# Scratch and queue places for the sums of the normed x in a decoder trunk on one core

## The chip, the cores and the metric

The kernel runs on one core of one Trainium2 chip. The metric is the device time of one execution in microseconds. Before the change it is 1301.23 us, the median of 3 runs (1300.35 to 1301.33). The engines are named as the profile names them: PE (TensorE, with PEld for its weight loads), DVE (VectorE), ACT (ScalarE), POOL (GpSimd) and SP (SyncE, whose queue issues the loads).

## The reference

Four sub-layers follow each other on a residual stream of 512 tokens and 1024 channels, all in float32: a gated MLP with position mixing, a squared-ReLU MLP, forgetting attention, and a second squared-ReLU MLP. The change touches the two squared-ReLU MLPs:

```python
h = rms_norm(x, mlp_norm_g[i])                      # x * rsqrt(mean(x*x)) * gain
x = x + jnp.square(jax.nn.relu(h @ w1)) @ w2         # w1: 1024 x 4096, w2: 4096 x 1024
```

## The kernel before

The stream is kept transposed: x is 8 tiles of 128 channels by 512 tokens. A float32 product is made of three matmuls of a reduced format: each operand is split into a high part (a copy that rounds, on ACT) and a low part (the remainder, on DVE), and high x high, high x low and low x high are added. Names that end in h and l are such parts: xh and xl of the normed x (without its scale per token), wh and wl of a chunk of weights, zh and zl of the MLP's inner activations.

**The norm.** Class Norm makes xh and xl of a block of x with its gain, squares the block on ACT (sq) and adds the squares up on POOL (sqs, line 283). When all 8 blocks are there, finish multiplies the sum by ones on PE (nps), and makes rstd on POOL (line 295); spread broadcasts rstd over the partitions with 4 matmuls (npb), copied by ACT to rbc. rbc is what the inner activations are scaled with.

**The MLP.** mlp handles w1 in pairs of chunks of 128 columns. The pairs 0 and 1 are made plainly (ph_0 to ph_3: 24 matmuls 512 wide for each chunk). nps stands after ph_1 and npb after ph_2 on PE. All later pairs are made by a scheme of 7 half-sized products instead of 8 (up_pair, PSUM tiles da and bc), in which two operands are needed as sums and differences:

- of the normed x: token_sums(k) for k = 0 to 3 takes the blocks k and k + 4 of x with gain (two copies on ACT, tx, line 466), makes four sums of 128 x 256 on POOL (ts, lines 470 to 473), and splits them (th on ACT, line 474; tl on DVE, line 475). They are made once for an MLP and serve all its pairs. Line 471 adds to the result of line 470, and line 473 to that of line 471.
- of the weights: Stream._sums makes four sums of 128 x 512 for each pair on POOL (ssum, lines 110 to 113) and splits them (sh, sl).

Both kinds of sums take their scratch from one tag, ssum, with two buffers: token_sums(k) takes both, one for tx and one for ts, and the sums of one pair of weights take both. The inner activations zh and zl have tags of their own with five buffers each.

Weights come through three raw buffers of 512 KB, loaded by SP in the order of use. A raw buffer is free for the next load when its split and its sums are made.

**What sets the order.** The kernel is written as a dataflow; a scheduler with a timeline of its own puts each engine's instructions in an order at build time, and every engine then works its own list in that order. Calls on keep_in_program_order pin a few matmuls (the first of ph_2 and of ph_3, and some in up_pair). In the program's text, token_sums stands after the plain pairs; the sums of weights of pair 2 come as soon as its chunks are asked for ahead of use.

## Time and profile before

| | |
|---|---|
| median of the runs | 1301.23 us |
| profiled execution, its own time | 1301.62 us |
| its span, first to last instruction | 1299.7 us |
| PE busy | 1273.0 us, 98% of the span |
| DVE, ACT, POOL busy | 867.9, 631.4, 511.3 us |
| PE's share of the chain that ended last | 85% |
| start of the first MLP in the span | about 289 us |
| start of the second MLP | about 941 us |

PE's busy time is modelled from pipelined matmuls and is no measure of its peak; the pace from one matmul's start to the next one's is. A row of the waits has the waiting engine and line, what it waited for, the sum in us, how many times, and the longest. A row of the chain has its start, its length and the engine, tile and line. A row of the timeline has start, duration, engine, line, operation, and in brackets the idle time before it with what ended it. The names there lack their numbers.

### The profile page before, as it was taken

Reading aid. Unit: us, or ns where it says so; the run is one execution under the profiler, and the core shown is the slowest. Engines: PE = TensorE matmul, PEld = TensorE weight load, DVE = VectorE, ACT = ScalarE, POOL = GpSimd, SP = SyncE. Lnnn points to the kernel's source line nnn. Section 1 sums busy time; section 2 is a strip of 40 time slices with the busy share of each in tenths; the row PEclk is TensorE's granted clock in tenths of the full one; section 3 lists DMA queues with packets and bytes.
Section 4 is the critical chain, followed back from the end, with each engine's and each line's share of the span. In section 5 each row is a group of like instructions: output and inputs, shape, how many; then the busy total and the mean of one; then the engine's idle time right before and its main releaser. Section 6 shows DMA issues by size and latency. Waiting matters only on the chain.

```text
span 1299.7 us, 18573 instructions
## 1 busy us (share of the span) xinstructions
PE 1273.0 (98%) x7204; PEld 1124.9 (87%) x7204; DVE 867.9 (67%) x1196; ACT 631.4 (49%) x992; POOL 511.3 (39%) x440
## 2 busy tenths in 40 slices
PE   9999999998999999999999999999988999999998
PEld 8888888887899999998899899998867999999987
DVE  7347767685676676766637777777875867676763
ACT  6234323255544343433467687787454534344430
POOL 4118533026433232310657567675285323222200
PEclk9999999999999999999999999999998999999999
DMA  6233232321332423233223222323212333332321
GB/s 240 88 111 98 82 94 85 97 83 49 115 114 80 130 79 117 90 106 94 75 83 102 81 82 79 93 68 112 81 49 84 113 112 96 100 111 85 114 82 65
DMA packets 39495, 124.01 MB, mean 95 GB/s; under 512 B 4688, under 2 KB 5728, under 8 KB 39408
## 3 DMA queue, kind: packets, MB, share of 16 engines
q1 hardware_dynamic: 39232, 122.82, 29.8%
q8 instruction: 56, 0.92, 0.3%
q14 instruction: 31, 0.25, 0.1%
q0 software_dynamic: 32, 0.02, 0.0%
q10 hardware_dynamic: 144, 0.00, 0.0%
HBM read 120.69 MB, written 2.13 MB: 95 GB/s over the span
## 4 chain that ended last, share of the span: by engine, by line
PE 85%; DVE 7%; POOL 3%; ACT 3%; issue 2%; DMA 0%; SPq 0%; POOLq 0%; DVEq 0%; ACTq 0%
PE po L241 34%; PE da L241 12%; PE bc L241 9%; PE pq L241 8%; PE pu L241 7%; PE pv L241 7%; PE pg L241 2%; DVE xl L269 2%; PE ot L241 2%; PE lg L241 1%; PE tp L246 1%; DVE wl L86 1%; PE sp L421 1%; DVE tl L475 1%; ACT wh L85 1%
## 5 line engine op out<-in xcount | busy, mean ns | idle before, releaser
L85 ACT ACTIVATE wh<-raw 128x1024 fp32r<-128x1024 f32 (+3 forms) x230 | 219.0, 953 | 284.2 <-PE po L241 80.8
L86 DVE TENSOR_TENSOR wl<-raw,wh 128x1024 fp32r<-128x1024 f32 (+1 forms) x178 | 250.5, 1419 | 75.2 <-ACT wh L85 73.4
L241 PE MATMUL po<-zl,wh 128*128 128x512 f32 x512 | 200.5, 392 | 0.0
L241 PE MATMUL po<-zh,wh 128*128 128x512 f32 x512 | 200.2, 391 | 0.0
L241 PE MATMUL po<-zh,wl 128*128 128x512 f32 x512 | 199.5, 390 | 0.0
L552 DVE TENSOR_TENSOR x<-x,po 128x512 f32<-128x512 f32 x128 | 87.3, 683 | 106.8 <-PE po L241 106.7
L86 POOL TENSOR_TENSOR wl<-raw,wh 128x768 fp32r<-128x768 f32 (+3 forms) x52 | 102.4, 1970 | 125.6 <-ACT wh L85 123.0
L110 POOL TENSOR_TENSOR ssum<-raw 128x512 f32<-128x512 f32 x28 | 38.1, 1359 | 246.2 <-DMA raw<-in_m_dram 216.7
L85 ACT ACTIVATE sh<-ssum 128x1024 fp32r<-128x1024 f32 x56 | 59.4, 1060 | 152.8 <-POOL ssum L111 112.1
L241 PEld LDWEIGHTS po<-zh,wl 128*128 128x128 f32 x512 | 96.3, 188 | 19.6
L241 PEld LDWEIGHTS po<-zh,wh 128*128 128x128 f32 x512 | 96.4, 188 | 18.0
L241 PEld LDWEIGHTS po<-zl,wh 128*128 128x128 f32 x512 | 96.5, 189 | 16.3
L241 PE MATMUL pq<-wh,xh 128*128 128x384 f32 (+2 forms) x256 | 88.4, 345 | 0.0
L405 POOL TENSOR_SCALAR vn<-v,mv,lnr 128x128 f32<-128x128 f32 x64 | 63.3, 1002 | 59.4 <-DVE vl L409 59.3
L241 PE MATMUL pq<-wh,xl 128*128 128x384 f32 (+2 forms) x256 | 83.1, 325 | 0.0
L241 PE MATMUL pq<-wl,xh 128*128 128x384 f32 (+2 forms) x256 | 82.7, 323 | 0.0
L86 DVE TENSOR_TENSOR sl<-ssum,sh 128x1024 fp32r<-128x1024 f32 x56 | 71.1, 1271 | 14.6 <-ACT sh L85 14.6
L112 POOL TENSOR_TENSOR ssum<-raw,ssum 128x512 f32<-128x512 f32 x28 | 42.2, 1507 | 78.4 <-DVE sl L86 78.2
L241 PE MATMUL da<-th,sl 128*128 128x256 f32 x224 | 63.4, 283 | 0.0
L241 PE MATMUL da<-tl,sh 128*128 128x256 f32 x224 | 63.4, 283 | 0.0
L241 PE MATMUL da<-th,sh 128*128 128x256 f32 x224 | 63.1, 282 | 0.0
L241 PE MATMUL pv<-wh,xl 128*128 128x512 f32 (+1 forms) x160 | 58.6, 372 | 0.5 <-DVE xl L269 0.5
(212 smaller groups left out, 3534.2 us busy)
## 6 DMA issues: line engine op xcount, KB each, us to landing
raw<-in_m_dram SPq DMA_DIRECT2D x128, 512.0 KB, 3.6
raw<-in_gw_u_dram SPq DMA_DIRECT2D x16, 512.0 KB, 3.5
raw<-in_gw_o_dram SPq DMA_DIRECT2D x16, 512.0 KB, 3.5
raw<-in_fw_qkv_dram SPq DMA_DIRECT2D x20, 384.0 KB, 3.0
raw<-in_gw_v_dram SPq DMA_DIRECT2D x14, 512.0 KB, 3.6
raw<-in_fw_g_dram SPq DMA_DIRECT2D x8, 512.0 KB, 3.4
cb<-cd SPq DMA_DIRECT2D x16, 256.0 KB, 3.3
raw<-in_fw_o_dram SPq DMA_DIRECT2D x8, 512.0 KB, 3.5
```

Source lines behind the costliest of these rows:

```text
L85: self.nc.scalar.activation(hi, t, AF.Copy)
L86: eng.tensor_tensor(lo, t, hi.bitcast(F32), op=ALU.subtract)
L110: tt(s12[:, 0], a21, a22, op=ALU.add)
L112: tt(s43[:, 0], a12, s12[:, 1], op=ALU.subtract)
L241: ins = pe.matmul(dst, a, b, start=start, stop=stop, skip_group_check=more)
L246: placed(pe.transpose(dst, src, ident[: src.shape[0], : src.shape[0]]), 256)
L269: dve.scalar_tensor_tensor(l, x[b], gcol, h.bitcast(F32), op0=ALU.mult, op1=ALU.subtract)
L405: pool.tensor_scalar(vn[:, i], v[i][:, cb * P : (cb + 1) * P], mv[:, i, 0:1], lnr[:, i : i + 1], op0=ALU.subtract, op1=ALU.mult)
L421: pe.matmul(dst, vh[:, 2 * c + i], wide, start=True, stop=False)
L475: dve.tensor_tensor(tl[k], t, th[k].bitcast(F32), op=ALU.subtract)
L552: dve.tensor_tensor(x[b], x[b], pt, op=ALU.add)
```

## The change

token_sums takes its two scratch tiles from the tags zh and zl (five buffers each) and no longer from ssum, so that the four rounds have eight tiles of their own. Its four rounds are moved in the text ahead of the plain pairs, and are queued behind the norm's last square on ACT and its last sum on POOL: issue_after(i) adds an edge of order, with no wait, from i to each instruction of the block that runs on i's engine. The first sums of weights after them are queued behind the last token sum on POOL in the same way.

```diff
-        self.sums_pool = None
+        self.sums_pool = self.sums_behind = None
...
         if kind == "second":
-            self._sums(i, self.raw.pop(i - 1)[0], t)
+            with self.sums_behind or nullcontext():
+                self._sums(i, self.raw.pop(i - 1)[0], t)
+            self.sums_behind = None
...
-            act.activation(sq, x[b], AF.Square)
+            self.squared = [act.activation(sq, x[b], AF.Square)]
...
-                pool.tensor_tensor(s, self.sum, sq, op=ALU.add)
+                self.squared.append(pool.tensor_tensor(s, self.sum, sq, op=ALU.add))
...
             def token_sums(k):
-                xg, t = (mp.tile([P, 2, S], F32, tag="ssum", name=f"t{w}{nm.n}_{k}", bufs=2) for w in "xs")
+                xg, t = (mp.tile([P, 2, S], F32, tag=f"z{w}", name=f"t{w}{nm.n}_{k}", bufs=5) for w in "hl")
...
-                tt(t[:, 3], b21, t[:, 1], op=ALU.subtract)
+                last = tt(t[:, 3], b21, t[:, 1], op=ALU.subtract)
                 act.activation(th[k], t, AF.Copy)
                 dve.tensor_tensor(tl[k], t, th[k].bitcast(F32), op=ALU.subtract)
+                return last
...
             zs = {}
+            with ExitStack() as behind:
+                for ins in nm.squared:
+                    behind.enter_context(tc.issue_after(ins.ins))
+                for k in range(4):
+                    last = token_sums(k)
+            ws.sums_behind = tc.issue_after(last.ins)
             phs = [up(0), up(1)]
             nm.finish()
...
             zs[1] = squares(1, more)
-            for k in range(4):
-                token_sums(k)
```

The change moves instructions on all engines at the start of each MLP; from the fourth pair on the lists are the same again. Three places matter here, all at the start of the first MLP.

POOL before, from the norm's last sum (sqs_7) into the second round of token sums. ssum are sums of weights, tx the x with gain, ts the sums:

```order
L283 TENSOR_TENSOR sqs_7_2452<-sqs_6_2430,sq_7_2450 128x512
L111 TENSOR_TENSOR ssum_0_2546<-ssum_0_2546,raw_2354 128x512
L112 TENSOR_TENSOR ssum_1_2547<-raw_2354,ssum_0_2546 128x512
L470 TENSOR_TENSOR ts_0_2639<-tx_0_2638 128x256
L472 TENSOR_TENSOR ts_0_2639<-tx_0_2638 128x256
L471 TENSOR_TENSOR ts_0_2639<-tx_0_2638,ts_0_2639 128x256
L295 TENSOR_TENSOR rstd_2537<-ms_2535,mhalf 128x4
L473 TENSOR_TENSOR ts_0_2639<-tx_0_2638,ts_0_2639 128x256
L470 TENSOR_TENSOR ts_1_2649<-tx_1_2648 128x256
```

And after the change, the end of the token sums (the scratch is now named th and tl as the split parts are, and is told from them by its 256 columns; lines from the second on are moved by 2):

```order
L475 TENSOR_TENSOR tl_0_2469<-th_0_2468,tl_0_2469 128x256
L472 TENSOR_TENSOR tl_3_2499<-th_3_2498 128x256
L474 TENSOR_TENSOR tl_3_2499<-th_3_2498 128x256
L473 TENSOR_TENSOR tl_2_2489<-th_2_2488,tl_2_2489 128x256
L475 TENSOR_TENSOR tl_1_2479<-th_1_2478,tl_1_2479 128x256
L473 TENSOR_TENSOR tl_3_2499<-th_3_2498,tl_3_2499 128x256
L475 TENSOR_TENSOR tl_2_2489<-th_2_2488,tl_2_2489 128x256
L297 TENSOR_TENSOR rstd_2577<-ms_2575,mhalf 128x4
L475 TENSOR_TENSOR tl_3_2499<-th_3_2498,tl_3_2499 128x256
L112 TENSOR_TENSOR ssum_0_2586<-raw_2404 128x512
```

sqs_7 now stands 8 token sums ahead of the first of these rows, with no sum of weights around it. The rounds are interleaved; the last sum of round 0 is the ninth of 16. rstd stands behind 15 token sums, where it stood behind three, and the sums of weights of pair 2 behind all 16. In the second MLP rstd stands behind 13, where it stood behind four.

ACT after the change, from the norm's last square (sq_7) to the copy of the broadcast rstd (rbc):

```order
L280 ACTIVATE sq_7_2450<-x_104 128x512
...
L468 ACTIVATE th_3_2498<-x_104,gains 128x512
L85 ACTIVATE wh_2542<-raw_2354 128x1024
L476 ACTIVATE th_0_2460<-tl_0_2469 128x1024
L85 ACTIVATE wh_2582<-raw_2404 128x512
L476 ACTIVATE th_1_2461<-tl_1_2479 128x1024
L476 ACTIVATE th_2_2462<-tl_2_2489 128x1024
L476 ACTIVATE th_3_2463<-tl_3_2499 128x1024
L85 ACTIVATE wh_2634<-raw_2509 128x1024
L306 ACTIVATE rbc_2629<-npb_2624 128x512
L85 ACTIVATE sh_0_2592<-ssum_0_2586 128x1024
```

The eight copies with gain follow sq_7 (seven of the eight are left out); before, sh_0 and sh_1 and a split of weights (wh) followed it, and the copies came two by two between the splits th. The splits of the sums of weights come after rbc now.

PE after the change, from the last matmul of ph_3 on:

```order
L243 MATMUL ph_3_2631<-xh_7_2446,wl_2512 128x512
L243 MATMUL da_2_2704<-th_0_2460,wh_2582 128x256
L243 MATMUL da_2_2704<-tl_0_2464,wh_2582 128x256
L243 MATMUL da_2_2704<-th_0_2460,wl_2583 128x256
L243 MATMUL da_2_2704<-th_1_2461,wh_2582 128x256
L243 MATMUL da_2_2704<-tl_1_2465,wh_2582 128x256
L243 MATMUL da_2_2704<-th_1_2461,wl_2583 128x256
L243 MATMUL da_2_2704<-th_2_2462,wh_2582 128x256
```

Pair 2's first product now runs through all four rounds; before, matmuls of bc_2 on xh and xl, and from there on of pair 3, stood between th_0 and th_1, and between th_1 and th_2.

## The prediction

> **What bounds the kernel now.** The page first: TensorE (PE) is busy nearly all of the span and holds most of the chain that ended last, so only a stretch in which PE stands still can give time back.

> ```profile
> span 1299.7 us, 18573 instructions
> PE 1273.0 (98%) x7204; PEld 1124.9 (87%) x7204; DVE 867.9 (67%) x1196; ACT 631.4 (49%) x992; POOL 511.3 (39%) x440
> ```

> Then the waits from 300 to 330 us, the start of the first MLP, and from the chain one round of what it names there:

> ```profile
> ACT th L474 <- POOL ts L473: 10.6, 4, 3.9
> POOL ts L470 <- DVE tl L475: 7.5, 3, 2.5
> PE da L241 <- ACT th L474: 5.2, 3, 4.0
> ...
> 309.77 0.74 POOL ts L470
> 310.52 0.70 POOL ts L472
> 311.21 1.70 POOL ts L471
> 312.97 0.75 POOL ts L473
> 313.74 1.07 ACT th L474
> 314.83 1.24 DVE tl L475
> ...
> 316.20 0.74 POOL ts L470
> ```

> PE waits for the split of the normed sums (th), that for POOL's sums (ts), and POOL for DVE's remainder (tl) of the last round: the scratch has two buffers and each round takes both, so the four rounds run one after another, 6.4 us each (309.77 to 316.20). What PE loses comes from the windows of PE alone (length, busy and count, clock, DMA), for both MLP starts, with its pace from the chain (12 narrow matmuls in 1.43 us, 17 wide ones in 3.89):

> ```profile
> 313.10:329.20 16.10, 9.95 (x55) 0.79 0.00 1
> 317.50:321.60 4.10, 0.07 (x1) 0.76 0.00 0
> 321.60:326.30 4.70, 4.69 (x22) 0.50 0.00 0
> 970.20:989.50 19.30, 13.47 (x86) 0.82 0.11 30
> 982.30:988.50 6.20, 5.86 (x25) 0.50 0.23 67
> ...
> 337.58 3.89 PE po L241 x17
> 341.70 1.43 PE da L241 x12
> ```

> All matmuls in the two long windows are narrow, 0.12 us each. First: 16.10 - 55 x 0.12 = 9.5 us lost. Second: 19.30 - 86 x 0.12 = 9.0. Part of it is no wait: after standing for 4 us PE ran at a granted clock of 0.50 for 4.70 us, where 22 matmuls should take 2.6 (2.1 lost).

> **The change, removed.** With a scratch tile for each round no round waits for the last one's tl, and all 16 sums follow each other. The ceiling is 9.5 + 9.0 = 18.5 us. The first real zh and zl take the fifth slots; the second pair takes slots free since tl_0, long before: nothing.

> **Moved on ACT.** Eight copies now stand right behind the last square. A pair took 1.32 us with its end, so eight take about 5. They fall into a hole, ACT's wait for the first sum of weights:

> ```profile
> 291.95 0.62 ACT L278 ACTIVATE sq<-x 128x512 f32<-128x512 f32 x1
> 298.33 1.06 ACT L85 ACTIVATE sh<-ssum 128x1024 fp32r<-128x1024 f32 x1 [5.76 <-POOL ssum L111]
> 301.61 1.32 ACT L466 ACTIVATE tx<-x,gains 128x512 f32<-128x512 f32 x2
> ```

> They end at 292.5 + 5 = 297.5, and the split of weights behind them, which before stood behind this sh and a second one, comes earlier. Without the hole it would be 5 us later. Cost: nothing.

> **Moved on POOL: the price.** The order shows that rstd, which PE needs for the broadcast npb, now stands behind 15 of the 16 sums in the first MLP and 13 in the second; before, behind 3 and 4. How long 15 sums take depends on DVE:

> ```profile
> 310.47 0.74 POOL L472 TENSOR_TENSOR ts<-tx 128x256 f32<-128x256 f32 x1
> 310.58 1.71 DVE L86 TENSOR_TENSOR wl<-raw,wh 128x1024 fp32r<-128x1024 f32 x1 [0.95 <-ACT wh L85]
> 311.17 1.73 POOL L471 TENSOR_TENSOR ts<-tx,ts 128x256 f32<-128x256 f32 x1
> 295.77 1.28 POOL L283 TENSOR_TENSOR sqs<-sqs,sq 128x512 f32<-128x512 f32 x1
> 305.56 1.02 POOL L295 TENSOR_TENSOR rstd<-ms,mhalf 128x4 f32<-128x4 f32 x1
> 306.64 0.60 PE L241 MATMUL npb<-ident,rstd 128*128 128x128 f32 x3 [0.32 <-POOL rstd L295]
> 291.41 1.54 DVE L86 TENSOR_TENSOR wl<-raw,wh 128x1024 fp32r<-128x1024 f32 x1
> ```

> A sum alone takes 0.70; DVE's wl began beside one, ended 1.1 after it, and the next sum ended 0.6 after that: the two engines take turns. So I walk the first start by turns. Last square done 292.6, wl done 292.95, sqs_7 (1.25) 294.2, xl_7 (0.6) 294.8, six sums 299.0, wl of the next chunk (1.1) 300.1, three sums 302.2: now round 0 is whole; th_0 (1.07) 303.3, meanwhile two sums 303.6, tl_0 (1.15) 304.75, one sum, half a wl (0.6), three sums 308.15. There tl_1 waits too. If rstd goes first it ends at 309.2, else at 310.3. PE reaches npb at 306.3, so it waits 2.9 to 4.0 and npb comes 2.6 to 3.7 later than at 306.64; I take 3.2.

> The second start has a cover for this:

> ```profile
> 944.94 1.85 DVE L269 SCALAR_TENSOR_TENSOR xl<-x,gains,xh 128x512 fp32r<-128x512 f32 x1
> 951.82 3.95 POOL L283 TENSOR_TENSOR sqs<-sqs,sq 128x512 f32<-128x512 f32 x2
> 955.82 1.05 PE L241 MATMUL nps<-ones,sqs 128*128 128x2 f32 x8 [1.47 <-POOL sqs L283]
> 963.91 0.83 PE L241 MATMUL npb<-ident,rstd 128*128 128x128 f32 x6
> ...
> PE ph L241 <- DVE xl L269: 1.6, 2, 0.9
> ```

> There the four sums of weights stood between the norm's squares and held sqs_7 to 955.8. With them behind, xl_5 (0.6 from 944.94) frees DVE and POOL at 945.6, and sqs_5, a wl, sqs_6, xl_6 and sqs_7 follow by turns (1.2 + 1.15 + 1.2 + 0.6 + 1.2) to 950.9. Then xl_7 (0.6), 13 sums (9.1), one and a half wl (1.75), perhaps tl_0 (1.15), and rstd (1.02), which ends at 963.4 or 964.5: npb stays within 0.6 of 963.91. PE, which waits less for xl and not for sqs_7, starts nps at about 953.2, and these (0.9) and 24 wide matmuls (5.5) bring it to npb at 959.6. It waits 3.9 to 4.9 there: the 4.3 us won ahead of npb are all given back. I take 0.

> **The clock after such a wait.** PE stood 2.0 us ahead of 975.30 and kept its clock, 3.5 ahead of 982.30 and 4.0 ahead of 321.6 and lost it:

> ```profile
> 975.30 0.39 PE L241 MATMUL da<-th,wh 128*128 128x256 f32 x1 [2.00 <-ACT th L474]
> 982.30 0.58 PE L241 MATMUL da<-th,wh 128*128 128x256 f32 x1 [3.50 <-ACT th L474]
> ```

> The new wait of the second start is over that bound: ph_3's wide matmuls at half clock for some 4.7 us lose about 2.2. That of the first lies astride it: I take half, 1.1. [...]

> **Sums of weights and loads, later.** The first sums of pair 2 stood here:

> ```profile
> 291.82 2.28 POOL L110 TENSOR_TENSOR ssum<-raw 128x512 f32<-128x512 f32 x1
> ```

> The four now start at about 310 and take some 7 us; their splits follow on ACT and DVE by 320.4. PE comes for them 36 narrow matmuls (4.3 us) after ph_3, at 319 or later. SP's loads of the next two chunks wait for them as well, where before one waited for a wl; they land 3.6 us after:

> ```profile
> raw<-in_m_dram SPq DMA_DIRECT2D x128, 512.0 KB, 3.6
> ```

> One place runs short: ACT's copy of an early product stands behind a split that waits for such a load, 0.6 us in each start by my walk. Without the cover of those 36 matmuls it would be 4.3 more.

> **Sum.** First 9.5 - 3.2 - 1.1 - 0.6 = 4.6. Second 9.0 - 0 - 2.2 - 0.6 = 6.2. Together 10.8 us off the profiled execution's 1301.62 (span 1299.7 and 1.9 around it), 1290.8; the median shown is 0.4 lower, so **1290.5**.

> **Rivals.** *rstd in time:* it goes ahead of tl_1 and the clock holds in both. First 9.5 - 2.6 - 0.6 = 6.3, second 9.0 + 0.5 - 0.6 = 8.9: 1286. For it: the short wait of the first start; against: 3.9 us in the second. With no turns taken at all (0.70 a sum) rstd ends at 305.7 and 961.0, the gains are 8.9 and 11.2, and the time is 1281, the lower bound.

> *Slower, POOL's queue ahead of npb:* with a mean of m us a sum, the first start gains 18.2 - 15m and the second 18.2 - 13m, half clock in both. At m = 1.73, the slowest row above, that is -7.8 and -4.3: 1313. It decides from m = 1.30. Against it, the 16 sums of each start as they ran:

> ```profile
> 302.30:326.80 24.50, 15.67 (x16) 0.86 0.14 43
> 956.90:981.20 24.30, 15.85 (x16) 0.93 0.14 44
> ```

> 0.98 and 0.99 each, which would give 9.0 and 1292. They had gaps in which DVE could work; now they have none.

> *The stall only changes its name:* m near 1.3, or PE runs dry at the sums of weights, 5 us in each start: about 1301. For it: POOL's work is the same. Against: POOL stood idle for 7.5 us between the rounds, and that goes.

> **How the numbers follow.** Forecast 0.66 (alone 1287 to 1294), rstd in time 0.20, name only 0.08, slower 0.06. The range reaches from near the bound without turns to just short of no change: 1283 to 1297. A measurement of this kernel can tell about 0.2%, 2.6 us: faster 0.86, same 0.08, slower 0.06.

> **What would show it.** Right: no wait of POOL for tl; both long windows full; PE waiting at npb for rstd, 3 to 4 us and 4 to 5 us, with a clock near 0.5 after the second. Wrong in the price: npb within 1 us of when ph_2 ends. Wrong altogether: waits of da or bc for sh or sl of 4 us and more in pairs 2 and 3, or rstd later than 312.

## The result and the profile after

The changed kernel takes 1291.23 us (median of 4 runs, 1290.36 to 1292.59) against 1300.79 us before (4 runs). The ratio is 0.9928, with a 95% interval of 0.9915 to 0.9940. The prediction was 1290.5 us, within 1283 to 1297.

From the page of the changed kernel, its span:

```profile
span 1290.8 us, 18568 instructions
```

The busy shares of the engines tell nothing of the change: PE has 98% as before. The waits of PE do, from 284 to 345 us, and behind the line of dots from 935 to 1000 us. (Lines of the code are two higher than before; tl on POOL's lines 472 to 475 is the scratch of the token sums, and th on ACT's line 468 is their x with gain.)

```profile
PE npb L243 <- POOL rstd L297: 3.1, 1, 3.1
PE po L243 <- ACT wh L85: 1.2, 1, 1.2
PE bc L243 <- ACT sl L526: 1.1, 1, 1.1
PE da L243 <- DVE zc L508: 0.4, 1, 0.4
...
PE npb L243 <- POOL rstd L297: 4.0, 1, 4.0
PE po L243 <- ACT wh L85: 0.7, 1, 0.7
```

PE's waits for th and tl are gone (for th 5.2 us in the part of the first start that was shown). In their place stands one wait for rstd in each start, 3.1 and 4.0 us, and in the first start three late ones, 2.7 us together.

The windows of PE alone show what these waits did to the clock: the wait and what stands behind it to the end of ph_3 in the first start, then the same in the second, with the part at half clock by itself (length, busy and count, clock, DMA).

```profile
305.96:309.04 3.08, 0.00 (x0) 1.00 0.00 0
309.04:315.51 6.47, 6.47 (x32) 1.00 0.15 36
956.29:960.30 4.01, 0.00 (x1) 0.89 0.00 0
960.30:966.01 5.71, 5.71 (x17) 0.50 0.00 0
960.30:969.58 9.28, 9.28 (x33) 0.68 0.17 49
```

Behind the wait of 3.08 us the clock stayed at 1.00. Behind that of 4.01 it was 0.50 for 5.71 us, and npb to the end of ph_3 took 9.28 us where it took 6.37 before (963.91 to 970.28).

Where the time came from is read by anchors on PE that both kernels have: the first ph of each MLP, and between them the first pq of the attention. The rows are PE's timeline, of before and then of the change:

```profile
288.88 0.39 PE L241 MATMUL ph<-xh,wh 128*128 128x512 f32 x1
644.88 0.35 PE L241 MATMUL pq<-wh,xh 128*128 128x400 f32 x1
941.12 0.39 PE L241 MATMUL ph<-xh,wh 128*128 128x512 f32 x1
```

```profile
288.52 0.39 PE L243 MATMUL ph<-xh,wh 128*128 128x512 f32 x1
641.05 0.34 PE L243 MATMUL pq<-wh,xh 128*128 128x400 f32 x1
937.73 0.39 PE L243 MATMUL ph<-xh,wh 128*128 128x512 f32 x1
```

| stretch | before | change | gain |
|---|---|---|---|
| ahead of the first MLP | 288.88 | 288.52 | 0.36 |
| first MLP | 356.00 | 352.53 | 3.47 |
| attention | 296.24 | 296.68 | -0.44 |
| second MLP to the end | 358.58 | 353.07 | 5.51 |
| span | 1299.7 | 1290.8 | 8.9 |

The new bound of the start is in the chain of waits of the change, from the norm's last sum to the third of the sums of weights of pair 2 (start, length, what):

```profile
292.37 1.37 POOL sqs L285
293.73 1.15 POOL tl L472
...
307.01 1.98 POOL rstd L297
...
313.45 2.25 POOL ssum L113
```

From 292.37 to 315.70 it is POOL, piece on piece with no gap. All engines in that stretch, of before and of the change (length; then busy and count of PE, PEld, DVE, ACT and POOL; clock, DMA):

```profile
293.70:326.00 32.30, 27.20 (x136) 23.09 (x135) 16.65 (x17) 17.51 (x22) 21.78 (x22) 0.90 0.16 49
```

```profile
293.70:326.00 32.30, 27.64 (x158) 23.74 (x157) 20.28 (x18) 16.69 (x23) 30.65 (x26) 1.00 0.16 50
```

POOL's busy time, its waits inside an instruction among it, went from 21.78 to 30.65 of 32.30 us. The engine that stood idle between the rounds has become the full one.

### The profile page after: what moved, and what is told of

Read it like the earlier page. It is cut to its first block, busy times and chain, and to the rows that moved or that the text cites. A ratio compares the mean times of both kernels' runs of the same rounds, so it can differ in the third digit from the quotient of the medians.

```text
span 1290.8 us, 18568 instructions
## 1 busy us (share of the span) xinstructions
PE 1269.8 (98%) x7204; PEld 1123.9 (87%) x7204; DVE 878.7 (68%) x1196; ACT 630.0 (49%) x992; POOL 515.1 (40%) x440
## 4 chain that ended last, share of the span: by engine, by line
PE 86%; DVE 5%; POOL 4%; ACT 3%; issue 1%; DMA 0%; POOLq 0%; ACTq 0%; DVEq 0%
PE po L243 34%; PE da L243 12%; PE bc L243 9%; PE pq L243 8%; PE pv L243 7%; PE pu L243 7%; PE pg L243 2%; DVE xl L271 2%; PE ot L243 2%; PE tp L248 1%; PE lg L243 1%; PE sp L423 1%; DVE ee L809 1%; ACT wh L85 1%; POOL tl L473 1%
## 5 line engine op out<-in xcount | busy, mean ns | idle before, releaser
L85 ACT ACTIVATE wh<-raw 128x1024 fp32r<-128x1024 f32 (+3 forms) x230 | 219.1, 953 | 282.1 <-PE po L243 85.3
L86 DVE TENSOR_TENSOR wl<-raw,wh 128x1024 fp32r<-128x1024 f32 (+1 forms) x178 | 256.4, 1453 | 59.9 <-ACT wh L85 59.4
L86 POOL TENSOR_TENSOR wl<-raw,wh 128x768 fp32r<-128x768 f32 (+3 forms) x52 | 102.4, 1969 | 126.4 <-ACT wh L85 123.8
L85 ACT ACTIVATE sh<-ssum 128x1024 fp32r<-128x1024 f32 x56 | 59.4, 1060 | 161.7 <-POOL ssum L113 116.8
L86 DVE TENSOR_TENSOR sl<-ssum,sh 128x1024 fp32r<-128x1024 f32 x56 | 72.6, 1296 | 9.9 <-ACT sh L85 9.8
L114 POOL TENSOR_TENSOR ssum<-raw,ssum 128x512 f32<-128x512 f32 x28 | 39.5, 1409 | 76.7 <-DVE sl L86 76.5
L115 POOL TENSOR_TENSOR ssum<-raw,raw 128x512 f32<-128x512 f32 x28 | 63.0, 2252 | 0.0
## 6 DMA issues: line engine op xcount, KB each, us to landing
raw<-in_m_dram SPq DMA_DIRECT2D x128, 512.0 KB, 3.6
raw<-in_gw_u_dram SPq DMA_DIRECT2D x16, 512.0 KB, 3.6
raw<-in_gw_o_dram SPq DMA_DIRECT2D x16, 512.0 KB, 3.6
raw<-in_gw_v_dram SPq DMA_DIRECT2D x14, 512.0 KB, 3.7
raw<-in_fw_g_dram SPq DMA_DIRECT2D x8, 512.0 KB, 3.4
raw<-in_fw_o_dram SPq DMA_DIRECT2D x8, 512.0 KB, 3.5
```

The costliest lines, as they stand in the source:

```text
L85: self.nc.scalar.activation(hi, t, AF.Copy)
L86: eng.tensor_tensor(lo, t, hi.bitcast(F32), op=ALU.subtract)
L114: tt(s43[:, 0], a12, s12[:, 1], op=ALU.subtract)
L115: tt(s43[:, 1], a11, a21, op=ALU.subtract)
```

## The experiments

**The theory** after the result: POOL's list from the norm's last sum (sqs_7) to pair 2's sums of weights sets both starts. Own scratch closes its gaps, the places in the queues bring it forward, and part of the gain is given back where rstd stands in that list. **The rivals:** one part of the change does it all; the wait for rstd is the only loss left; POOL's long instructions have nothing to do with DVE.

**The scratch alone** (against the kernel before):

```diff
-                xg, t = (mp.tile([P, 2, S], F32, tag="ssum", name=f"t{w}{nm.n}_{k}", bufs=2) for w in "xs")
+                xg, t = (mp.tile([P, 2, S], F32, tag=f"z{w}", name=f"t{w}{nm.n}_{k}", bufs=5) for w in "hl")
```

> The scratch alone: each round of token sums has tiles of its own (as in the change), but the four rounds stand at their old place in the program's text and nothing is queued behind anything. The scheduler now puts the eight sums of weights of pairs 2 and 3 ahead of all 16 token sums in POOL's list, and rstd ahead of them. Theory (own scratch ends the serial rounds, the places in the queue bring the sums forward, and both are needed): npb on time as before (within 0.5 us of before in both starts), no POOL wait for tl, but the token sums begin only near 310 and 971 us; PE stands 4 to 9 us for th_0 in each start with half clock behind it; about 1297 us (1293 to 1303). Rival (the scratch carries the gain, the queue places are needed for nothing): with rstd not delayed it would be as good as the change or better, 1284 to 1291.

Measured: 1312.02 us, ratio 1.0084 (1.0069 to 1.0099): slower than before. The rival is out, and the time is 9 us beyond the upper end expected. PE's long wait in the first start (the second has one of 11.4 us), then the first token sum on POOL and the copies on ACT that it waits for:

```profile
323.91 0.58 PE L241 MATMUL da<-th,wh 128*128 128x256 f32 x1 [11.85 <-ACT th L474]
...
318.21 1.15 POOL L470 TENSOR_TENSOR tl<-th 128x256 f32<-128x256 f32 x1 [5.81 <-ACT th L466]
...
317.42 3.77 ACT L466 ACTIVATE th<-x,gains 128x512 f32<-128x512 f32 x6
```

The sums began at 318.2 us, not at 310, because ACT came to the copies of x with gain only at 317.4, behind the rectified activations of two pairs. The expectation had looked at POOL's list alone. With its own scratch no round waits for another one, and the scheduler put all of them late. So the place in ACT's queue counts too, and not only that in POOL's; what each is worth alone was not measured.

**The queue places alone:** the change with token_sums on its old scratch (tag ssum, two buffers).

> The places in the queues alone: token sums behind the norm's last square and last sum, first sums of weights behind them, but the scratch is the old one of two buffers. Theory: rounds run one after another again, about 5.1 to 6.4 us each, but from 293.7 and 947.4 on, so that the last of them ends near 314 and 970; rstd stands behind 8 and 4 sums, and npb is not late (no PE wait over 1 us there). What is lost comes later: the sums of weights of pair 2 begin 5 to 7 us later than in the change and PE waits 3 to 5 us for their splits or for th_3, in each start. About 1295 us (1291 to 1299). Rival (the serial rounds were the cause, so with two buffers nothing is won): 1300 to 1302. Rival (the queue places carry all): 1291 or less.

Measured: 1297.25 us, ratio 0.9968 (0.9957 to 0.9980), inside what was expected. npb did not wait; POOL's rounds stood apart again, as its row of round 3 shows, and PE waited for th of the last round, 4.5 us in the second start:

```profile
312.34 0.73 POOL L472 TENSOR_TENSOR ts<-tx 128x256 f32<-128x256 f32 x1 [2.50 <-DVE tl L477]
...
971.57 0.58 PE L243 MATMUL da<-th,wh 128*128 128x256 f32 x1 [4.50 <-ACT th L476]
```

The places win 3.9 us of the median, the scratch alone loses 10.9, both together win 9.6. The two parts are one change.

**Without the last edge** (the change, with the sums of weights free again):

```diff
-            ws.sums_behind = tc.issue_after(last.ins)
```

> The change without its last edge: the first sums of weights are not queued behind the token sums and go back to where the scheduler puts them, two of the four ahead of the norm's last square sum and two among the token sums; rstd stands behind 11 token sums and three or four sums of weights in the first start, behind 8 and none in the second (there the four stand between the norm's sums). Theory (what is queued on POOL ahead of rstd sets npb): first start npb near 313, some 4 us later than in the change, with half clock behind it, but fewer late waits (the 2.7 us of po, da and bc shrink to about 1); second start sqs_7 late again by some 4 us, npb on time for that, no half clock behind it. About 1293 us (1290 to 1298). Rival (where the four sums of weights stand makes no difference): 1290 to 1292, with npb in both starts as in the change.

Measured: 1295.63 us, ratio 0.9958 (0.9942 to 0.9975). The first start's npb came at 312.21 (313 expected) after a wait of 6.25 us, and the second's without a wait but 24.6 us behind its first ph (939.27), where the change has 22.6:

```profile
312.21 2.08 PE L243 MATMUL npb<-ident,rstd 128*128 128x128 f32 x8 [6.25 <-POOL rstd L297]
```

So the last edge is worth some 4 us (4.4 between the medians): what stands on POOL ahead of rstd sets npb, be it token sums or sums of weights.

**rstd between the rounds:** the change, with rounds 2 and 3 of the token sums behind rstd on POOL.

```diff
                 for k in range(4):
-                    last = token_sums(k)
-            phs = [up(0), up(1)]
-            nm.finish()
+                for k in range(2):
+                    token_sums(k)
+                phs = [up(0), up(1)]
+                nm.finish()
+                with tc.issue_after(nm.made.ins):
+                    for k in range(2, 4):
+                        last = token_sums(k)
+            ws.sums_behind = tc.issue_after(last.ins)
```

> The change with rounds 2 and 3 of the token sums queued behind rstd on POOL: rstd now stands behind 8 sums in both starts instead of 15 and 13. Theory (a second queue of nearly the same length stands behind the first: the sums of weights begin no earlier, because POOL's work ahead of them is the same): rstd by 302 and 956, PE's waits of 3.1 and 4.0 us for it and the half clock of the second start go, but PE then comes 3 to 6 us earlier to the splits of pair 2's sums of weights (in the change they were done 1.3 to 1.7 us ahead of PE) and waits there for most of it, 1 to 2 us in the first and 4 to 5 in the second. About 1288 us (1285 to 1290). Rival (the wait for rstd was lost time with nothing behind it): the 3.1 + 4.0 us and the 2.9 us of half clock all come off: 1281 to 1283. Rival (POOL's order is of no account): 1291.

Measured: 1288.93 us, ratio 0.9908 (0.9893 to 0.9923). npb came 3.2 us earlier in the first start and 5.2 in the second (306.18 and 954.16, counted from the first ph at 288.90 and 936.74), but of the 8.4 us only 3.0 are left at the anchors: 1.3 in the first MLP and 1.7 in the second. PE's main wait of the first start:

```profile
PE da L243 <- DVE tl L477: 1.7, 2, 1.4
```

and the second, by three rows of PE's timeline:

```profile
962.65 0.39 PE L243 MATMUL da<-th,wh 128*128 128x256 f32 x1 [1.14 <-ACT th L476]
964.57 0.39 PE L243 MATMUL da<-tl,wh 128*128 128x256 f32 x1 [0.94 <-DVE tl L477]
966.80 0.58 PE L243 MATMUL da<-tl,wh 128*128 128x256 f32 x1 [1.37 <-DVE tl L477]
```

The time is the one expected and the place was another: PE now meets the splits of rounds 2 and 3, not those of the sums of weights. The wait for rstd had work of almost its own length behind it; the rival that took it for plain loss (1281 to 1283) is out. This kernel and the change were run again side by side:

> The same kernel as the run with rstd between the rounds, now in five rounds beside the change on the same chip, to tell 1288.9 from 1291.2 us: if rstd's place is worth what the traces show (a span of 1288.1 against 1290.8), the ratio to before is 0.991 and lies 0.15 to 0.25% below the change's; if the two are the same, both come out at 0.992.

> The change itself in five rounds, beside the run with rstd between the rounds: 1290 to 1292.5 us, a ratio to before of 0.992 to 0.993.

Measured: 1288.74 us (1288.54 to 1289.45), ratio 0.9910 (0.9894 to 0.9925), and 1290.97 us (1290.57 to 1292.05), ratio 0.9926 (0.9914 to 0.9939). The intervals overlap, the runs do not: every run of this kernel lies below 1289.9 and every run of the change itself above 1290.3. It is the fastest kernel here that makes the whole product, 2.2 us below the change.

**The wait filled:** the change, and in the second start ahead of npb

```diff
+            if n == 3:
+                with tc.issue_after(order["last"].ins):
+                    for i in range(6):
+                        mm(pb, self.h[0][:, :P], self.h[1], True, True)
```

> The change, and in the second start six wide matmuls on xh whose result is thrown away (they write npb's bank ahead of npb), queued behind the last matmul of ph_2, where PE waits for rstd: 6 x 0.227 = 1.4 us of the 4.0 us are filled. The list of work behind npb differs a little on ACT, DVE and PE, because the scheduler reckons with the six. Theory (the half clock behind npb comes from PE standing for 4.0 us, while 3.1 us in the first start cost nothing): the wait shrinks to 2.6 us, npb starts at the same place (22.6 us after the first ph of that MLP), the granted clock stays 1.0 behind it, and npb to the end of ph_3 takes 6.4 us instead of 9.3; about 1288.5 us if the 2.9 us stay won, 1291 if PE only meets the sums of weights earlier. Rival (the clock falls for another reason, by the load of the stretch): clock 0.5 behind npb again, 9.3 us.

Measured: 1296.05 us, ratio 0.9961 (0.9949 to 0.9974). PE alone from the six matmuls to npb, then from npb to the end of ph_3, in windows; below them PE's next row of the timeline:

```profile
956.09:960.35 4.26, 1.52 (x7) 1.00 0.00 0
960.35:966.80 6.45, 6.45 (x32) 1.00 0.00 0
```

```profile
971.71 0.58 PE L243 MATMUL da<-th,wh 128*128 128x256 f32 x1 [4.72 <-DVE zc L512]
```

PE stood for 2.75 us here, the clock stayed at 1.00, and 6.45 us took the place of 9.28. That fits the theory, but it is one execution, and a wait of 1.87 us in the attention of the change was followed by half clock (0.50 from 723.90 to 727.32); the last section has what PE did in the steps ahead of each half clock. The time did not follow, because the small difference in the lists behind npb has zc on DVE behind two splits tl, where the change has it ahead of them, and the first of the two took 4.38 us (1.23 undisturbed):

```profile
964.47 4.38 DVE L481 TENSOR_TENSOR tl<-tl,th 128x1024 fp32r<-128x1024 f32 x1 [1.72 <-ACT th L480]
```

PE waited 4.7 us for zc. What the half clock alone is worth in the whole is not shown by this run.

**All sums on DVE** (the change, with one word):

```diff
-                tt = pool.tensor_tensor
+                tt = dve.tensor_tensor
```

> The change with all 16 token sums made on DVE instead of POOL (so the edge behind the norm's last POOL sum binds nothing, and the sums of weights stand where the scheduler puts them: two of the first four ahead of sqs_7 in the first start, all four ahead of it in the second). A sum of half the width of zc's two-operand row on DVE (0.68 us for 512 columns) should take 0.35 us: 16 x 0.35 = 5.6 us on DVE instead of 16 x 0.72 = 11.5 us on POOL. Theory (POOL's queue from sqs_7 to pair 2's sums of weights, some 22 us, is what sets both starts): no PE wait for rstd over 1 us, no half clock behind npb; in the first start nearly the whole 9.5 us come off; in the second sqs_7 is late again by some 4 us, the window of 9.0 us is full. About 1285 us (1282 to 1288). Rival (DVE becomes the bound: ms, wl and tl stand behind 16 sums there): waits of ph or da for wl or tl of 3 us and more, 1291 or above.

Measured: 1294.45 us, ratio 0.9951 (0.9935 to 0.9966). The theory's time was missed by 9 us and the rival was right in part: PE waited 8.8 us for rstd in the first start. A sum does run faster on DVE (0.41 us against 0.73), but look at rstd (DVE's row is the end of a run that began at 308.4, behind ms, and has no gap):

```profile
311.82 1.81 DVE L86 TENSOR_TENSOR wl<-raw,wh 128x512 fp32r<-128x512 f32 x2
...
308.58 5.96 POOL L297 TENSOR_TENSOR rstd<-ms,mhalf 128x4 f32<-128x4 f32 x1 [8.99 <-DVE ms L295]
```

ms, behind DVE's new backlog, began 8 us after the end of nps (3.5 in the change), and then rstd, an instruction of 1.03 us elsewhere, took 5.96 and ended 0.9 us after DVE's run.

**All sums on DVE, the sums of weights behind the norm's last sum:**

```diff
-            ws.sums_behind = tc.issue_after(last.ins)
+            ws.sums_behind = tc.issue_after(nm.squared[-1].ins)
```

> As the run before, with the first four sums of weights queued behind the norm's last sum on POOL (and not behind the token sums), so that they no longer hold sqs_7 in the second start; rstd stands behind them, 4 sums of weights instead of 13 or 15 token sums. Theory: npb on time within 2 us in the first start (4 x 1.3 to 2.3 us from 294 on end near 302, but ms stands behind the token sums on DVE), and in the second npb 22 us or less after the first ph without a wait over 1 us, so that the 4 us ahead of npb stay won. About 1282 us (1279 to 1286), better than both. Rival (DVE is the bound): 1288 to 1291 with PE waiting for tl or sl.

Measured: 1302.66 us, ratio 1.0014 (1.0005 to 1.0023), 20 us above what was expected. In the first start rstd took 5.95 us. In the second it took 8.21, again to 0.9 us behind the end of DVE's run, and PE waited 12.1:

```profile
964.10 8.21 POOL L297 TENSOR_TENSOR rstd<-ms,mhalf 128x4 f32<-128x4 f32 x1 [6.72 <-DVE ms L295]
970.22 1.21 DVE L86 TENSOR_TENSOR wl<-raw,wh 128x1024 fp32r<-128x1024 f32 x1
```

**What is locked out?** All sums on DVE, and one small addition ahead of each rstd:

```diff
+            probe = small.tile([P, NT], F32, tag="probe", name=f"probe{n}", bufs=1)
+            pool.tensor_tensor(probe, self.ms, mhalf[:, :NT], op=ALU.add)
             pool.tensor_tensor(self.rstd, self.ms, mhalf[:, :NT], op=ALU.pow)
```

> All token sums on DVE, as in the run before of that kind, and ahead of each rstd on POOL one addition of the same small size (128 x 4, the same two operands, its result used by nobody). There rstd took 5.96 us instead of 1.03 and ended 0.9 us after the end of an unbroken run of DVE instructions that began just before it, while sums of 128 x 512 on POOL took turns with DVE's, one for one. Theory (what is locked out is any POOL instruction that arrives when DVE runs without a gap): the addition starts near 308.6 and ends only when DVE pauses, near 314, and rstd behind it takes its usual 1.0. Rival (it is the power function that is locked out, because it needs DVE's side for its whole length): the addition ends within 1.5 us, between two DVE instructions, and rstd takes 4 us and more. The time itself tells nothing; about 1294 to 1296 us in both cases.

Measured in one execution: 1300.27 us, above the 1294 to 1296 expected; no run here says why.

```profile
310.35 5.12 POOL L298 TENSOR_TENSOR probe<-ms,mhalf 128x4 f32<-128x4 f32 x1 [9.00 <-DVE ms L295]
315.43 1.03 POOL L299 TENSOR_TENSOR rstd<-ms,mhalf 128x4 f32<-128x4 f32 x1
```

The addition is held up in the place of rstd (5.12 us), and rstd takes its usual time (1.03): it is not the power function that is locked out.

**Round 0 on DVE**, rounds 1 and 2 on POOL ahead of rstd, round 3 behind it:

```diff
-                tt = pool.tensor_tensor
+                tt = eng.tensor_tensor
...
-                for k in range(2):
-                    token_sums(k)
+                for k in range(3):
+                    token_sums(k, dve if k == 0 else pool)
...
-                    for k in range(2, 4):
+                    for k in range(3, 4):
```

> The change with round 0 of the token sums on DVE, which stands idle when they begin (294 to 298 us), rounds 1 and 2 on POOL ahead of rstd, and round 3 on POOL behind rstd; the sums of weights behind all. Theory (what sets both starts is POOL's queue from the norm's last sum to pair 2's sums of weights; four sums less are some 3 to 4 us less): rstd stands behind 8 sums as in the run with rstd between the rounds, where npb was on time, and the sums of weights begin some 3 us earlier than there (309 and 959 instead of 312.1 and 962.1), so that the waits of 1.7 + 0.2 + 0.9 us of the first start and of 2.3 + 1.1 + 0.3 us of the second go for the most part: about 1285 us (1283 to 1288). Rival (DVE late instead: ms and wl stand behind four more instructions there, and rstd is locked out by DVE): npb waits 2 us and more again, 1289 to 1293. Rival (the waits of that run have another cause): 1288 to 1290.

Measured: 1293.15 us, ratio 0.9936 (0.9923 to 0.9950): slower than with all rounds on POOL. PE's largest waits of the second start, and below them, from the timeline, POOL's first and last sum ahead of rstd in the first:

```profile
PE npb L243 <- POOL rstd L297: 2.7, 1, 2.7
PE po L243 <- DVE wl L86: 1.9, 1, 1.9
```

```profile
294.20 0.93 POOL L472 TENSOR_TENSOR tl<-th 128x256 f32<-128x256 f32 x1 [0.48 <-ACT th L468]
302.71 1.60 POOL L475 TENSOR_TENSOR tl<-th,tl 128x256 f32<-128x256 f32 x1
```

The eight sums took 10.1 us (294.20 to 304.3) where with all rounds on POOL they took 7.6 (293.98 to 301.6). Work moved from POOL to DVE came back as POOL's waiting: the sums of weights began only 1.3 and 1.7 us earlier, counted from nps, not 3, and DVE's own splits were late. The rival "DVE late instead" came nearest: its time (1289 to 1293) was just passed, and npb waited in the second start only.

**One operand:**

```diff
-                dve.tensor_tensor(tl[k], t, th[k].bitcast(F32), op=ALU.subtract)
+                dve.tensor_scalar(tl[k], t, 0.0, None, op0=ALU.mult)
```

> The change with one thing left out of the computation: the low parts of the token sums are set to zero by an instruction with one operand (t times 0) where DVE subtracted th from t, two operands. So DVE has as many instructions in the same places, but those four read one tile instead of two. The order differs in one place that matters here: rstd stands behind 14 token sums in the first start instead of 15. Theory (a token sum or rstd of 1.7 to 2.0 us is one that waits for a DVE instruction with two operands): beside tl nothing is stretched any more; the sum that took 1.72 beside tl_0 in the first start takes 0.73 and rstd 1.0 instead of 2.02 and 2.00; rstd ends near 306.3 in the first start (308.99 less 1.0 less 1.0 less 0.7) and near 959.2 in the second (960.24 less 1.0), counted with the first ph at 288.5 and 937.7. Only sums beside wl and xl are still stretched. Rival (POOL's long instructions have another cause, as the sums' own order): rstd 2.0 us and a stretched sum near 302.8 again; rstd ends at 308.3 and 960.2.

Measured in one execution: 1288.25 us. rstd ended at 307.4 and 957.8 us with the first ph at 288.70 and 935.84, so 307.2 and 959.7 by the change's count: halfway between theory and rival, in both starts. POOL beside tl_0, then rstd of the first start, then DVE's tl beside POOL and alone:

```profile
302.26 1.18 POOL L474 TENSOR_TENSOR tl<-th 128x256 f32<-128x256 f32 x1
305.95 1.48 POOL L297 TENSOR_TENSOR rstd<-ms,mhalf 128x4 f32<-128x4 f32 x1
...
301.64 1.22 DVE L477 TENSOR_SCALAR tl<-tl 128x1024 fp32r<-128x1024 f32 x1 [2.00 <-POOL tl L475]
956.89 0.69 DVE L477 TENSOR_SCALAR tl<-tl 128x1024 fp32r<-128x1024 f32 x1 [0.61 <-POOL tl L475]
```

The instruction with one operand takes 0.69 us alone, the one with two 1.23, and POOL beside it was stretched by 0.45 instead of 1.0. So DVE is the cause, and the stretch went down with the length of DVE's instruction; the theory that one operand leaves POOL alone is wrong.

## Why the prediction was right, step by step

The forecast (POOL's rounds closed up, npb late in the first start and not in the second, half clock behind the longer wait) is what happened. Term by term, in us, by the anchors above:

| term | predicted | measured |
|---|---|---|
| first start: full window | 9.5 | 9.5 (the ceiling, taken over, not measured by itself) |
| npb later | -3.2 | -2.8 (309.04 - 288.52 against 306.64 - 288.88) |
| half clock | -1.1 | 0 (clock 1.00) |
| late waits | -0.6 | -3.3 (what is left to 3.47; the waits on the list are 2.7) |
| second start: full window | 9.0 | 9.0 (the ceiling, taken over) |
| npb | 0 | +0.2 (960.30 - 937.73 against 963.91 - 941.12) |
| half clock | -2.2 | -2.9 (9.28 against 6.37) |
| late waits | -0.6 | -0.8 (what is left to 5.51; the wait on the list is 0.7) |
| both starts | 10.8 | 9.0 |

**The walk by turns** held in the main. A mean token sum took 0.89 us in the first start (15 from 293.69 to 306.97) and 0.84 in the second (13 from 947.35 to 958.24). The sums that stretch to 1.70 each stand beside a DVE instruction. These means are under the 0.98 and 0.99 of before and far under the 1.30 at which the rival "POOL's queue ahead of npb" would have decided. Counted from the first ph, the walk had the fifteenth sum end 0.8 us later than it did (19.27 against 18.45), and rstd take 1.0 us less than it did. So npb's place in the first start is partly luck: two errors that nearly cancel. rstd began beside tl on DVE and took 2.02 us instead of 1.03, 1.0 us more, as the sum that began beside tl_0 did (1.72 us at 302.78 instead of 0.73):

```profile
306.97 2.02 POOL L297 TENSOR_TENSOR rstd<-ms,mhalf 128x4 f32<-128x4 f32 x1
306.76 2.60 DVE L477 TENSOR_TENSOR tl<-tl,th 128x1024 fp32r<-128x1024 f32 x2 [1.72 <-ACT th L476]
```

**The term that was mis-sized** is the last of the part on the sums of weights and loads, "One place runs short", 0.6 us in each start. In the first start 3.3 us are left for it. Three waits on PE's list make 2.7 of them: po for wh, da for zc, bc for sl; for the other 0.6 no wait was found. The prediction had looked for PE's wait at the sums of weights, which were in time (sl_0 ended at 318.1, PE came at 319.8). It had not walked DVE behind rbc. There the sums of weights of pairs 2 and 3, moved to 309.9 to 325.7, stretch DVE's instructions between them:

```profile
312.21 2.31 DVE L86 TENSOR_TENSOR wl<-raw,wh 128x1024 fp32r<-128x1024 f32 x1
320.58 2.30 DVE L499 TENSOR_TENSOR zl<-zc,zh 128x1024 fp32r<-128x1024 f32 x1
```

An undisturbed one of this width takes 1.21 to 1.23. That these longer instructions make the three waits is read from the trace, and for po it is least sure: by the profile its wh on ACT had waited for PE's own bc, and zl, which po takes next, was done 0.3 us after it. No run took those turns away alone.

**The clock.** The second start went as forecast: 4.0 us of standing and half clock behind it. But the prediction's bound (2.0 us kept, 3.5 lost) is no bound on the length of a wait. Every wait of 3.5 us and more in the traces of before and of the change (3.50, 4.0 and 4.01 us) was followed by half clock, and so were 4.02 us in another execution of the change and 8.8 us with all sums on DVE. Of the shorter ones, 3.08 us and 2.75 us (the wait filled) were not, while 1.87 us (the change itself, in the attention, at 723.68) was; at the same place before, 1.90 us (at 727.62) was not. The kernel before had half clock without a long wait too: from 957.9 to 961.3, where no wait ahead was over 1.5 us. The prediction took half of 2.2 us for the first start because it could not tell; that this wait kept its clock (it did in both profiled executions of the change, 1.00 from 293.70 to 326.00) was luck for the sum. The 1.1 charged there came back, which hid 1.1 us of the 2.7 that the mis-sized term was short.

**The other rivals.** "rstd in time" needed no turns; 3.1 and 4.0 us of waiting rule it out. "The stall only changes its name" is out for the change, and right for what comes after it: the run with rstd between the rounds won 8.4 us at npb and kept 3.0.

## What to carry to other kernels

When a chain of rounds is serialised by scratch, count the whole list of the engine that makes them, up to the next thing that anyone waits for: with the gaps closed that list is the new bound, and a short instruction that another engine needs (rstd here) belongs ahead of the last rounds, not behind them (here 1288.93 us against 1291.23). Own buffers alone let a scheduler put work late (here 1312.02 us against 1300.79), so say where it is queued on every engine that it uses, the one that prepares its operands too. Between VectorE and GpSimd, work moved from one to the other was not free of the first here (eight sums on GpSimd took 10.1 us with round 0 on VectorE, 7.6 without): price the two together.

## What the runs showed that was not expected

```profile
304.06:307.47 3.41, 1.90 (x9) 1.00 0.00 0
307.47:310.88 3.41, 1.84 (x12) 1.00 0.00 0
956.01:959.42 3.41, 0.28 (x2) 1.00 0.00 0
720.49:723.90 3.41, 1.54 (x11) 1.00 0.25 77
```

The first start's wait of 3.08 us lies across two steps, and PE was busy for over half of each. The 4.01 us of the second start empty one step. In these two traces a step at full clock in which PE was busy for 0.41 of it or less was always followed by half clock (0.41 and 0.13 before, 0.08 in the change, 0.00 at both ends), one of 0.65 and more never, and between them both happened (0.45 and 0.61 were followed by half clock, 0.46 and 0.52 to 0.59 were not). Several short waits did it as well: in the second execution of the kernel with rstd between the rounds PE waited 1.16, 0.94 and 1.36 us within 5.3 us, and the clock from 960.30 to 969.58 was 0.82 in the mean, with a narrow matmul every 0.21 us behind the third wait where it is 0.12. How the filled wait lay to the steps is not shown.
- **The same wait does not always cost the same.** In another execution of the change, PE waited 4.02 us for rstd in the second start, and behind it the half clock lasted 2.77 us (0.50 from 959.73 to 962.50) where it had lasted 5.71: it had one step of the grid there and two here. npb to the end of ph_3 took 7.8 us there instead of 9.3, a spread of 1.5 us between executions that no edit makes.
